# Second half of a feed-forward: weight pairs that move on one by one, stored sums added by accumulating transfers, epilogues in the following visit

## The chip, the cores and the metric

The kernel runs on one core of a Trainium2 chip. The core has a matrix engine (TensorE, PE in the profile, with its weight loads as PEld), VectorE (DVE), ScalarE (ACT), GpSimd (POOL) and SyncE (SP), which here issues nearly all transfers. The metric is the device time of one execution in microseconds; lower is better. The time before is the median of three runs.

## The reference

One layer of a hybrid encoder block: 16 learned tokens are put ahead of 2048 tokens of width 1024; three mixers (a gated linear recurrence, a forgetting attention and an RWKV-7 group) read one input projection and end in one output projection; then comes the feed-forward, which the change is about:

```python
f = causal_dwconv(rms_norm(h, norm_ffn_pre[l]) @ ffn_up[l], ffn_conv[l])
gate, val = jnp.split(f, 2, axis=-1)
f = (jax.nn.gelu(gate, approximate=True) * val) @ ffn_down[l]
h = h + rms_norm(f, norm_ffn_post[l])
```

`ffn_up` is 1024 x 5632, `ffn_down` 2816 x 1024, all in float32; the first 16 rows are dropped at the end.

## The kernel before

The stages follow one another: input projection with the recurrences beside it, attention, output projection (`w_out_tile`), the up half of the feed-forward (`ffn_up`, three passes over 684 tokens each, 22 units a pass), and the down half (class `Down`). Every matrix product is made from a high and a low part of its operands in fp32r: `mm3` (L170) issues three matmuls, high x high, high x low, low x high, on lines 172 to 174. `split` (L1601) makes the parts: ACT copies the high one, DVE or POOL subtracts to get the low one.

**Up.** A unit of `ffn_up` makes 128 gate and 128 value columns with seven products of a Winograd-like scheme. They share three banks of PSUM; `conv` (L1733) reads a finished sum three times, in the bank itself for three of the four outputs, once on ACT (L1736) and twice on DVE (L1738), and `ending` (L1743) multiplies on POOL and stores to the scratch `ff`. `between` (L2137) runs beside each unit: at unit 14 of the last pass (`DOWN_FROM`) it prepares the down weights of the first pair.

**Down.** `ffn_down` has 22 blocks of 128 rows. Twenty of them make ten pairs, k = 0 to 9 (`DOWN_PAIRS`), each worked as 2 x 2 blocks with seven products; the last two blocks (the remaining pair) are multiplied plainly. For a pair, `down_operands` (L1820) loads seven 128 x 512 weight operands, four of them sums kept in the scratch `ds`, and splits each into a slot of 4 KB a partition. Here a set means the seven operands of one pair. Slots: nine in `qp` (the tile `qd` in the profile, kept from the space of the up half's inputs) and 26 in a ring of three pools (tile `dw`, `DOWN_SLOTS`, `DOWN_TURNS`): 35 slots, five sets.

The 2048 tokens make eight blocks of 256. The first half visits every block with pairs 0 to 4, the second half visits every block again with pairs 5 to 9 and the remaining pair. So there are sixteen visits (`Down.pair`, L1867). In each, for each pair, `side` (L1844) loads a 256 x 256 piece of `ff` (tile `u`), POOL makes four sums of 128 x 128 (L1856 to L1859), ACT and DVE split the seven pieces (tile `fo`), and TensorE issues 21 matmuls into seven banks (tile `psd`). Tiles `u` and `fo` have two buffers. At the end of a visit ACT copies three banks (`la`, `rb`, `lb`), DVE makes the sums (L1891 to L1895) and adds the other banks (L1904). `la`, `ra`, `lb`, `rb` and `u2` have one buffer each.

`first` (L1907) stores the four 128 x 512 results to the scratch `part`. `second` (L1914) loads them back (tile `pt`), POOL adds them (L1901), and then `add_normed` (L1510) makes the norm: two squares with row sums on ACT (L1516), the root, then on DVE y x rstd x gain (L1525) and the add to h (L1526); the result goes to `out`. All of this stands at the end of the visit to which it belongs.

The framework orders each engine's instructions with a planner that works from the order of the text and modelled times; `issue_after(ins)` puts instructions behind `ins` in the queue of the same engine. Each engine works its queue in order, and SP's waits hold up the transfers queued behind them.

## Time and profile before

| | us |
|---|---|
| median of three runs | 3062.89 (3059.62 to 3063.98) |
| the profiled execution | 3063.42 |
| its span, first to last instruction | 3061.7 |
| last matmul of the up half starts (in the span) | 2592.2 |
| first matmul of the down half | 2592.3 |
| last matmul of the down half ends | 3050.6 |

The page gives the busy time of each engine over the whole span, and then what each engine did in 40 slices. This line of it shows the load of the transfer engines, in GB/s for each slice; the last six slices are the down half:

```profile
GB/s 216 244 234 207 163 240 292 154 199 205 211 156 92 88 105 211 109 100 122 75 94 206 171 181 180 172 202 213 209 215 212 220 192 165 171 102 175 148 162 145
```

In the views that follow, L172 is line 172 of the kernel, `psd<-dw,fo` is output from inputs, `x416` a count, and a bracket such as `[3.57 <-DVE uy L1738]` is idle time of the engine before the instruction and what ended it. Timelines give start and duration in us from the start of the span.

### The profile page before, as it was taken

What the parts mean: (1) busy time and instruction counts of PE and PEld (TensorE: products, weight loads), DVE (VectorE), ACT (ScalarE), POOL (GpSimd) and SP (SyncE); (2) the same over time, 40 slices, a digit from 0 to 9 for tenths busy, and PEclk for the clock granted to TensorE, in tenths of its full rate; (3) what the DMA queues carried; (4) which work ended last, traced back from release to release, by engine and by line L of the source; (5) the groups of instructions that cost most, each with busy time, mean ns of one, the idle gap of its engine ahead of it and who ended that gap; (6) DMA issues with size and microseconds to landing.
All of it is one profiled execution on the core that took longest, in us unless ns stands there. A gap on an engine that the chain in (4) does not pass through costs nothing.

```text
span 3061.7 us, 52809 instructions
## 1 busy us (share of the span) xinstructions
PE 2910.2 (95%) x18694; PEld 2487.6 (81%) x18694; DVE 2057.7 (67%) x3934; ACT 1479.1 (48%) x2853; POOL 1365.7 (45%) x1599
## 2 busy tenths in 40 slices
PE   6998999999989999999999899999999999999998
PEld 6997898888876654566568899999999999787786
DVE  5268645656677785555636888888778777547766
ACT  4245332434346554454534656666566665324333
POOL 1001121122214556566843457445645544556765
PEclk8999999999989898999999999999999999999999
DMA  6776478466654347434336555566677765535454
GB/s 216 244 234 207 163 240 292 154 199 205 211 156 92 88 105 211 109 100 122 75 94 206 171 181 180 172 202 213 209 215 212 220 192 165 171 102 175 148 162 145
DMA packets 467750, 532.58 MB, mean 174 GB/s; under 512 B 85550, under 2 KB 355576, under 8 KB 465932
## 3 DMA queue, kind: packets, MB, share of 16 engines
q1 hardware_dynamic: 466716, 528.27, 56.5%
q8 instruction: 147, 2.41, 0.3%
q14 instruction: 119, 0.97, 0.1%
q0 software_dynamic: 768, 0.93, 0.1%
HBM read 369.11 MB, written 159.95 MB: 173 GB/s over the span
## 4 chain that ended last, share of the span: by engine, by line
PE 34%; DVE 5%; DMA 5%; POOL 3%; issue 3%; ACT 1%; SPq 0%; POOLq 0%; DVEq 0%; ACTq 0%
PE psu L172 8%; PE psu L173 8%; PE psu L174 8%; PE psd L172 2%; PE psd L173 2%; PE psd L174 2%; DMA u<-scr_ff 2%; DMA xt<-scr_h 1%; DVE uw L1603 1%; PE pswo L172 1%; PE pswo L174 1%; PE pswo L173 1%; DVE fo L1603 1%; DVE uy L1738 1%; POOL u L1858 1%
## 5 line engine op out<-in xcount | busy, mean ns | idle before, releaser
L172 PE MATMUL psu<-xo,uw 128*128 128x344 f32 x1848 | 590.8, 323 | 14.7 <-DVE vb L1787 6.9
L173 PE MATMUL psu<-xo,uw 128*128 128x344 f32 x1848 | 593.1, 321 | 0.0
L174 PE MATMUL psu<-xo,uw 128*128 128x344 f32 x1848 | 584.3, 320 | 1.5 <-DVE uw L1603 1.5
L172 PE MATMUL psp<-xh,wh 128*128 128x384 f32 (+2 forms) x1152 | 383.5, 333 | 4.5 <-ACT wh L166 3.0
L174 PE MATMUL psp<-xh,wl 128*128 128x384 f32 (+2 forms) x1152 | 379.5, 330 | 2.6 <-DMA wl<-scr_wk 2.5
L173 PE MATMUL psp<-xl,wh 128*128 128x384 f32 (+2 forms) x1152 | 379.3, 329 | 0.0
L1603 DVE TENSOR_TENSOR uw<-uq,uw 128x512 fp32r<-128x512 f32 x341 | 321.0, 947 | 65.1 <-ACT uw L1602 62.8
L172 PEld LDWEIGHTS psu<-xo,uw 128*128 128x128 f32 x1848 | 347.4, 189 | 19.2 <-DVE vb L1787 9.4
L174 PEld LDWEIGHTS psu<-xo,uw 128*128 128x128 f32 x1848 | 347.2, 189 | 2.4 <-DVE uw L1603 2.3
L173 PEld LDWEIGHTS psu<-xo,uw 128*128 128x128 f32 x1848 | 348.5, 189 | 0.1
L1602 ACT ACTIVATE uw<-uq 128x512 fp32r<-128x512 f32 x462 | 287.5, 627 | 107.5 <-PE psu L174 46.6
L686 ACT ACTIVATE p<-sc,bias 128x512 f32<-128x512 f32 (+4 forms) x352 | 197.0, 589 | 194.9 <-PE sc L682 162.1
L559 DVE TENSOR_REDUCE mc<-mx 128x1 f32<-128x512 f32 (+6 forms) x352 | 190.2, 564 | 114.1 <-PE mx L554 87.2
L1738 DVE SCALAR_TENSOR_TENSOR uy<-psu,ffn_cols,uy 128x342 f32<-128x342 f32 (+1 forms) x396 | 223.7, 567 | 62.3 <-ACT uy L1736 60.9
L1744 POOL TENSOR_TENSOR uy<-uy,uy 128x342 f32<-128x342 f32 (+1 forms) x132 | 140.0, 1061 | 252.7 <-DVE uy L1738 70.1
L725 POOL TENSOR_TENSOR acc<-acc,p 128x512 f32<-128x512 f32 (+3 forms) x208 | 221.7, 1068 | 53.1 <-DVE acc L725 23.9
L1603 POOL TENSOR_TENSOR uw<-uq,uw 128x512 fp32r<-128x512 f32 x121 | 177.6, 1468 | 148.0 <-ACT uw L1602 129.5
L172 PEld LDWEIGHTS psp<-xh,wh 128*128 128x128 f32 x1152 | 221.7, 192 | 11.6 <-issue 4.2
L174 PEld LDWEIGHTS psp<-xh,wl 128*128 128x128 f32 x1152 | 220.8, 192 | 12.0 <-issue 5.7
L173 PEld LDWEIGHTS psp<-xl,wh 128*128 128x128 f32 x1152 | 221.3, 192 | 7.5 <-issue 5.4
L1603 DVE TENSOR_TENSOR fo<-u,fo 128x896 fp32r<-128x896 f32 x88 | 109.0, 1240 | 118.8 <-ACT fo L1602 118.8
L1602 ACT ACTIVATE fo<-u 128x896 fp32r<-128x896 f32 x88 | 81.1, 922 | 200.9 <-POOL u L1859 103.8
(470 smaller groups left out, 6470.3 us busy)
## 6 DMA issues: line engine op xcount, KB each, us to landing
uq<-scr_us SPq DMA_DIRECT2D x220, 256.0 KB
uq<-in_ffn_up_dram SPq DMA_DIRECT2D x209, 256.0 KB
wl<-scr_wk SPq DMA_DIRECT2D x48, 512.0 KB
wh<-scr_wk SPq DMA_DIRECT2D x48, 512.0 KB
u<-scr_ff SPq DMA_DIRECT2D x88, 256.0 KB
scr_ff<-uy SPq DMA_DIRECT2D x110, 171.0 KB
raw<-in_w_in_dram SPq DMA_DIRECT2D x24, 512.0 KB
scr_wk<-wh SPq DMA_DIRECT2D x24, 512.0 KB
```

What stands on the lines that cost most here:

```text
L172: nc.tensor.matmul(out, ah, bh, start=first, stop=False, skip_group_check=more)
L173: nc.tensor.matmul(out, ah, bl, start=False, stop=False, skip_group_check=more)
L174: nc.tensor.matmul(out, al, bh, start=False, stop=last, skip_group_check=more)
L559: self.reduced = nc.vector.tensor_reduce(mc[:rows, i, ci : ci + 1], ps[:rows, : e - a], axis=AX.X, op=ALU.max)
L686: last = nc.scalar.activation(p[:rows, :w], ps[:rows, :w], AF.Exp, bias=bias[:rows, j : j + 1])
L725: eng.tensor_tensor(a, ps_[0][0][:rows, c0:n] if start and i == 1 else a, p[:rows, : n - c0], op=ALU.add)
L1602: core.nc.scalar.activation(hi, src, AF.Copy)
L1603: (eng or core.nc.vector).tensor_tensor(lo, src, hi, op=ALU.subtract)
L1738: stt(y[:, :n], src[:, i : n + i], cw[:, 44 * i + cc : 44 * i + cc + 1], y[:, :n], op0=ALU.mult, op1=ALU.add)
L1744: core.pooled = nc.gpsimd.tensor_tensor(v[:, :n], g[:, :n], v[:, :n], op=ALU.mult)
L1858: tt(s3, a0, b0, op=ALU.subtract)
```

## The change

Six things change, all at or after the end of the up half.

1. `down_visits`: visit `pair` of the first half works on the five pairs from 5 x pair // 8 on, the second half on the other five, modulo ten. The sets that a visit needs therefore move on by one pair at most from a visit to the next. Fourteen sets are prepared in all (ten before). The following visit's new set is prepared by `ahead`, which is called behind the third side of a visit.
2. 35 slots as before, but ten of them are filled before the down half (three operands of the second pair too, at units 13 and 17 of the last pass): the tenth is the space of `g_fpre`, whose pool `gf` is now opened earlier. The other 25 lie in five pools in another order. The splits of sets 2 and 3 are put behind the last ACT and DVE work of `conv` (`DOWN_HELD`).
3. In the last up unit the sums of two products are written to SBUF tiles instead of to their banks, and the last product is copied to SBUF before `conv`.
4. First half: the stores to `part` are queued behind the load of the fifth following side.
5. Second half: no load of `part`, no adds on POOL. Four transfers issued by POOL add the stored sums onto `la`, `ra`, `lb` and `rb` behind the third following side; norms follow behind the fourth, stores to `out` behind the sixth. The last visit adds the stored sums within its own epilogue. `add_scaled` multiplies by the gain before the root is known, then does (y x rstd) + h in one pass.
6. The remaining pair's weights are loaded in visit 7 (`DOWN_REST`).

```diff
+def add_scaled(core, pool, halves, gain, x, junk):
+
+    nc = core.nc
+    v = pool.tile([P, 8], F32, tag="rs2", name=core.n("rs2"))
+    sums = v[:, 4:5], v[:, 5:6]
+    for y, acc in zip(halves, sums):
+        nc.scalar.activation(junk, y, AF.Square, accum_out=acc)
+    for c, y in enumerate(halves):
+        nc.vector.tensor_tensor(y, y, gain[:, 512 * c : 512 * c + 512], op=ALU.mult)
+    r1 = rstd_root(core, v, sums, D)
+    for c, y in enumerate(halves):
+        xc = x[:, 512 * c : 512 * c + 512]
+        nc.vector.scalar_tensor_tensor(xc, y, r1, xc, op0=ALU.mult, op1=ALU.add)
...
-DOWN_SLOTS = 5, 13, 8
-DOWN_TURNS = (2, 3), (0, 5), (1, 13), (2, 5)
-DOWN_FROM = 14
+DOWN_SLOTS = 5, 7, 1, 2, 10
+DOWN_TURNS = (3, 2), (4, 5), (0, 5), (4, 5), (1, 7), (2, 1)
+DOWN_FROM = 13, 17
+DOWN_HELD = 2, 4
+DOWN_REST = 6
+DOWN_AHEAD = 2
+DOWN_STORED = 5
+DOWN_PARTS, DOWN_NORMS, DOWN_OUT = 3, 4, 6
...
             elif name == "p3":
-                tt(ps, ps, u2, op=ALU.add)
-                gb = conv(ps, 0, j, n[1])
+                sum_ = ps if more else u2
+                tt(sum_, ps, u2, op=ALU.add)
+                gb = conv(sum_, 0, j, n[1])
...
             elif name == "p2":
-                tt(ps, ps, ga, op=ALU.add)
-                ga = conv(ps, 0, j, n[0])
+                sum_ = ps if more else ga
+                tt(sum_, ps, ga, op=ALU.add)
+                ga = conv(sum_, 0, j, n[0])
...
             else:
-                va = conv(ps, 1, j, n[0])
+                src = ps
+                if not more:
+                    src = s("ga")
+                    nc.scalar.activation(src, ps, AF.Copy)
+                va = conv(src, 1, j, n[0])
...
+def down_visits(pairs):
+
+    for half in range(2):
+        for pair in range(pairs):
+            first = DOWN_CUT * pair // pairs + DOWN_CUT * half
+            yield half, pair, range(first, first + DOWN_CUT)
...
+        self.sides += 1
+        while self.due and self.due[0][0] <= self.sides:
+            with core.tc.issue_after(load.ins):
+                self.due.pop(0)[1]()
+        return side
...
-        for k in ks:
-            side, w = self.side(k, pair), weights(k)
+        for i, k in enumerate(ks):
+            if i == DOWN_AHEAD:
+                self.due.insert(0, (self.sides + 1, ahead))
+            side, w = self.side(k % DOWN_PAIRS, pair), weights(k)
...
-        for i, row in enumerate(((lb, rb), (la, ra)) if rest else ()):
-            t0 = P * (2 * pair + i)
-            pt = self.spool.tile([P, D], F32, tag="hx", name=core.n("pt"))
-            nc.sync.dma_start(pt[:], self.scr["part"][t0 : t0 + P, :])
-            for c, y in enumerate(row):
-                nc.gpsimd.tensor_tensor(y, y, pt[:, 512 * c : 512 * c + 512], op=ALU.add)
+        out = (la, ra), (lb, rb)
+        if between:
+            between(*out)
...
+        self.after(DOWN_STORED, lambda: store(1, a))
+        self.after(DOWN_STORED, lambda: store(0, b))
...
+        def parts(*ab):
+            for i, halves in zip((1, 0), ab):
+                t0 = P * (2 * pair + i)
+                for c, y in enumerate(halves):
+                    part = self.scr["part"][t0 : t0 + P, 512 * c : 512 * c + 512]
+                    nc.gpsimd.dma_start(y, part, accum_op=ALU.add)
+
+        a, b, junk = self.pair(pair, ks, weights, ahead, rest, parts if ends else None)
...
+        def norms():
+            for t0, halves in rows:
+                hx = self.spool.tile([P, D], F32, tag="hx", name=core.n("hx"))
+                nc.sync.dma_start(hx[:], self.scr["h"][META + t0 : META + t0 + P, :])
+                add_scaled(core, self.spool, halves, self.gain, hx, junk)
+                sums[t0] = hx
...
+        if not ends:
+            self.after(DOWN_PARTS, lambda: parts(a, b))
+        self.after(DOWN_NORMS, norms)
+        self.after(DOWN_OUT, stores)
...
+            def ahead(pair=pair, half=half, ks=ks, last=following[2][-1]):
+                if last not in ks:
+                    weights(last)
+                if half == 0 and pair == DOWN_REST:
+                    for i in range(2):
+                        rest.append(dwn.tile([P, 2, D], F32R, tag=f"r{i}", name=core.n("dwn")))
+                        at = P * (2 * DOWN_PAIRS + i)
+                        load_parts(core, (dpo, "hx", None), a["ffn_down"][at : at + P, :], rest[i][:, 0], rest[i][:, 1])
```

More of the change, by code (lines that the diff above doesn't have):

```diff
@@ L2193, in hybrid_block_kernel @@
+        down[:0] = [dws[i] for i, n in DOWN_TURNS for _ in range(n)]
         steps = Down(core, dpo, dpf, dpe, ps_d, scr, g_fpost, out)
         pairs = SEQ // (2 * P)
[L2195 to L2203 removed]
@@ L2215, in hybrid_block_kernel, with weights @@
-        rest = []
-        for pair in range(pairs):
-            steps.second(pair, ks[1], weights, last)
+        ended = core.taken.ins, core.conved.ins
+        def weights(c):
+            have = ws.setdefault(c, [])
+            if len(have) < len(DOWN_PRODUCTS):
+                raw = lambda: dwr.tile([P, 512], F32, tag="dq", name=core.n("raw"))[:]
+                with ExitStack() as behind:
+                    for ins in ended if c in range(*DOWN_HELD) else ():
+                        behind.enter_context(tc.issue_after(ins))
+                    some = range(len(have), len(DOWN_PRODUCTS))
+                    have += down_operands(core, raw, slot, a["ffn_down"], scr, c % DOWN_PAIRS, some)
+            return have
@@ new lines, in hybrid_block_kernel @@
+        rest = []
+        def last():
+            return rest
+        visits = list(down_visits(pairs))
+        for (half, pair, ks), following in zip(visits, visits[1:] + visits[-1:]):
+            def ahead(pair=pair, half=half, ks=ks, last=following[2][-1]):
[6 more added lines that the diff above has]
+                        load_parts(core, (dpo, "hx", None), a["ffn_down"][at : at + P, :], rest[i][:, 0], rest[i][:, 1])
+            if half == 0:
+                steps.first(pair, ks, weights, ahead)
+                if pair == 1:
+                    gain = a["norm_ffn_post"].rearrange("(o n) -> o n", o=1).broadcast_to([P, D])
+                    nc.sync.dma_start(g_fpost[:], gain)
+            else:
+                steps.second(pair, ks, weights, ahead, last, (half, pair, ks) == visits[-1])
@@ L2220 @@
+        steps.finish()
 def kernel(**inputs):
```

122 lines of the change are left out of this document (58 added, 64 removed).

## The prediction

> **What bounds the kernel now.** I read the totals first, then the second half of the feed-forward cut into its visits. A visit is one of the 16 passes of the down projection over 256 tokens; the first eight take 105 matmuls each (5 weight pairs, 7 products, 3 matmuls), the last eight 129 (24 more for the remaining pair of row blocks). The view of windows below is cut at visit 1, visits 2 to 7, visit 8, visit 9, visits 10 to 16, and the tail after the last matmul. Its columns are window, length, then busy time of each engine with its count, granted clock, DMA share and rate.
>
> ```profile
> PE 2910.2 (95%) x18694; PEld 2487.6 (81%) x18694; DVE 2057.7 (67%) x3934; ACT 1479.1 (48%) x2853; POOL 1365.7 (45%) x1599
> 2592.00:2628.20 36.20, 29.78 (x109) 21.81 (x107) 25.45 (x28) 20.22 (x33) 22.19 (x25) 0.86 0.75 250
> 2628.20:2774.30 146.10, 145.43 (x631) 118.66 (x632) 70.56 (x82) 39.47 (x51) 76.96 (x122) 1.00 0.32 107
> 2774.30:2799.50 25.20, 24.68 (x106) 19.31 (x104) 21.84 (x22) 14.27 (x24) 20.10 (x20) 1.00 0.62 206
> 2799.50:2837.60 38.10, 32.78 (x129) 25.93 (x130) 32.31 (x34) 18.27 (x29) 27.94 (x31) 0.91 0.55 179
> 2837.60:3050.60 213.00, 210.23 (x904) 168.66 (x903) 147.63 (x192) 72.28 (x136) 143.87 (x165) 1.00 0.47 155
> 3050.60:3061.70 11.10, 0.00 (x0) 0.00 (x0) 6.59 (x14) 2.40 (x8) 0.76 (x1) 0.59 0.38 142
> ```
>
> TensorE bounds the kernel, here as elsewhere. Visits 2 to 7 are six times 105 matmuls in 146.1 us, 0.2319 us each, with PE busy throughout: that is the pace at which nothing is missing. At it a visit of the first half takes 24.35 us, one of the second half 29.9. So the losses are: visit 1, 36.2 - 24.35 = 11.85; visit 8, 0.85; visit 9, 38.1 - 29.9 = 8.2; visits 10 to 16, 213.0 - 7 x 29.9 = 3.6. Together 24.5 us, which is all that a rearrangement of these visits can win, plus something of the 11.1 us tail. The number of matmuls does not change.
>
> Visit 1, in the timeline of PE:
>
> ```profile
> 2592.79 0.40 PE L174 MATMUL psd<-qd,fo 128*128 128x512 f32 x1
> 2596.76 0.77 PE L172 MATMUL psd<-qd,fo 128*128 128x512 f32 x1 [3.57 <-DVE uy L1738]
> ...
> 2599.72 0.76 PE L172 MATMUL psd<-qd,fo 128*128 128x512 f32 x1 [1.34 <-DVE uy L1738]
> 2600.29 0.63 PE L173 MATMUL psd<-qd,fo 128*128 128x512 f32 x1
> ...
> 2604.98 0.63 PE L172 MATMUL psd<-qd,fo 128*128 128x512 f32 x1
> 2605.71 0.39 PE L174 MATMUL psd<-qd,fo 128*128 128x512 f32 x1
> ```
>
> Two banks of PSUM are still being read by the convolutions of the last up unit (4.9 us of waiting), and then 11 matmuls from 2600.29 to 2604.98 start 0.426 us apart: half clock. Seventeen such matmuls, at 0.194 above the pace, cost 3.3 us. The remaining 3.65 us are weights and sides that come late.
>
> **The change, part by part.** *Start-up.* In the last up unit the two sums now go to SBUF tiles and the last product is copied there, so a bank is held for one add or one copy, not for a scaling and two more passes. Rows of the tile psu in the stretch from 2570 to 2600:
>
> ```profile
> L1738 DVE SCALAR_TENSOR_TENSOR uy<-psu,ffn_cols,uy x14: 558/566/574, 2569.8 to 2599.0; 128x342 f32<-128x342 f32 x10, 128x338 f32<-128x338 f32 x4
> L1736 ACT ACTIVATE uy<-psu,ffn_cols x6: 522/530/545, 2573.6 to 2593.2; 128x342 f32<-128x342 f32 x4, 128x338 f32<-128x338 f32 x2
> L1768 ACT ACTIVATE u<-psu x2: 458/458/458, 2571.2 to 2584.2; 128x344 f32<-128x344 f32 x2
> L1790 DVE TENSOR_TENSOR psu<-psu,ga x2: 515/520/524, 2574.7 to 2590.2; 128x344 f32<-128x344 f32 x2
> ```
>
> Each of three banks comes free 0.53 + 2 x 0.57 = 1.67 us of work earlier, against one more copy of 0.46, which lies under the matmuls; with ACT and DVE queues in between I take both waits as gone, and with them the slow stretch. Then weights become the limit. Ten of the 35 operands of visit 1 are now ready before it (seven before), and the remaining pair's load (two transfers of 512 KB) leaves the rush:
>
> ```profile
> 2596.00:2608.00 12.00, 9.89 (x27) 7.43 (x28) 8.34 (x11) 7.22 (x11) 5.74 (x5) 0.60 0.92 314
> L1602 ACT ACTIVATE dw<-raw x26: 612/629/637, 2589.7 to 2618.3; 128x512 fp32r<-128x512 f32 x26
> L1603 DVE TENSOR_TENSOR dw<-raw,dw x18: 678/692/1781, 2590.9 to 2619.1; 128x512 fp32r<-128x512 f32 x18
> L1603 POOL TENSOR_TENSOR dw<-raw,dw x8: 1259/1294/1721, 2594.0 to 2620.3; 128x512 fp32r<-128x512 f32 x8
> L166 ACT ACTIVATE dwn<-raw x2: 1056/1056/1057, 2601.6 to 2603.6; 128x1024 fp32r<-128x1024 f32 x2
> L167 DVE TENSOR_TENSOR dwn<-raw,dwn x2: 1226/1226/1226, 2602.7 to 2604.7; 128x1024 fp32r<-128x1024 f32 x2
> ```
>
> In that window the transfers run at a 0.92 share and 314 GB/s: they are the limit. Three operands of 256 KB and two of 512 KB are 1.84 MB, 5.8 us at that rate; 2.1 us of ACT and 2.5 of DVE go with them, in the same queues. So the weights come 5.8 us earlier, and a little more where the ACT or DVE queue was the holder: I take 6.5 of the 11.85. Ends: 0 (the weights were late anyhow) and 11.85.
>
> The Trainium skill (TensorE: Matmul & The Clock Gate, "Part 1: The HAM clock gate") has the clock fall after an idle window of about 3.4 us. By that rule any remaining wait shorter than that is free of the slow stretch, and visit 1 could win 3.3 us more. Visit 9 disagrees: there waits of 2.81 and 1.31 us, the first for ACT, bring the granted clock to 0.72 in the 12 us from 2800. So I do not count on it.
>
> ```profile
> 2800.00:2812.00 12.00, 8.42 (x24) 6.36 (x25) 12.00 (x13) 8.28 (x15) 10.97 (x12) 0.72 0.86 281
> 2802.27 0.50 PE L172 MATMUL psd<-qd,fo 128*128 128x512 f32 x1 [2.81 <-ACT fo L1602]
> 2804.79 1.22 PE L174 MATMUL psd<-qd,fo 128*128 128x512 f32 x2 [1.31 <-DVE fo L1603]
> ```
>
> *The seam.* Before, all five sets of weights are exchanged while visits 8 and 9 run: DVE is busy 12.00 of 12 us in the window above, and the sides (fo) queue behind 25 splits. Now each visit replaces at most one set: prepared in visits 2, 4, 5, 7, 8, 10, 12, 13 and 15, nine sets, four more than before (28 operands, 7 MB). Such a set takes seven ACT splits, 7 x 0.629 = 4.4 us, five on DVE, 3.5 to 8.9, and two on POOL, 2.6. Its slots come free after the first pair of the visit and it is wanted at the last pair of the next one, some 40 us later, so arrival is not the question; delay of the sides in the queues is. In the first half DVE has 70.56 / 6 = 11.8 us of 24.35: room. Bounds for one set: 0, and the 0.85 of visit 8, in which a first part of the sets was prepared. I take 0.3, nearer to visits 2 to 7, whose DVE has twice the room that visit 8 had: 5 x 0.3 = 1.5 us in the first half.
>
> *The second half.* Visits 10 to 16 lose 0.5 each, through this chain (tables of waits of PE's loads and of DVE from 2838 to 3051):
>
> ```profile
> PEld psd L172 <- ACT fo L1602: 6.7, 11, 1.0
> DVE ra L1904 <- POOL ra L1901: 8.8, 7, 1.4
> L1901 POOL TENSOR_TENSOR la<-la,pt x8: 1293/1738/1747, 2836.1 to 3043.9; 128x512 f32<-128x512 f32 x8
> L2041 POOL DMA_DIRECT2D scr_p<-zeros x12: 537/537/720, 1.3 to 10.4; - x12
> DMA to landing us min/median/max: 2.9/5.7/6.7
> ```
>
> The stored sums are added by POOL, about 1.74 + 3 x 1.27 = 5.6 us a visit (the smaller value is a row of the tail, below), between the adds that make the sides; DVE waits for them, and ACT's split waits for both. The change takes these adds off POOL and puts four accumulating transfers in their place. No such transfer is in the trace. The nearest are POOL's twelve small stores at the start: 0.54 us to issue, 2.9 to 6.7 to land. So POOL gives 2.2 us in place of 5.6. The norms move into the next visit, behind its fourth side. Same operations in number, but there DVE has to fit a weight set too: 147.63 / 7 = 21.1 us a visit, plus 3.5 to 8.9, of 29.9. That eats what the shorter chain gives, so I leave 0.5 us of loss in each of the eight visits, visit 9 now included: 4.0 in place of 11.8, -7.8 us. Ends: 0 lost (-11.8), and nothing won beyond the seam's own 8.2 given back by crowded visits (0).
>
> *The tail.* The last visit cannot spread its epilogue. Rows of POOL, DVE and SP:
>
> ```profile
> 3050.09 1.27 POOL L1901 TENSOR_TENSOR rb<-rb,pt 128x512 f32<-128x512 f32 x1
> 3051.40 0.69 DVE L1904 TENSOR_TENSOR rb<-rb,psd 128x512 f32<-128x512 f32 x1
> 3056.97 0.69 DVE L1526 TENSOR_TENSOR hx<-hx,rb 128x512 f32<-128x512 f32 x1
> ```
>
> Before, rb is complete at 3052.1. Now its transfer is issued about 3049.5 and lands 2.9 to 6.7 later, 3052.4 to 3056.2, and DVE's add follows: 1 to 4.8 us late. In return the gain is multiplied in while ACT squares, and the other row is finished by then; from 3052.1 to 3057.7 the old chain interleaves both rows in 5.6 us, the new one needs about 3 after rb. Between -1.6 and +2.2: I take 0.
>
> *Sum.* -6.5 (visit 1) - 0.85 (visit 8) - 7.8 (second half) + 1.5 (sets) + 0 (tail) = -13.65 us. The profiled execution took 3063.42 us (its span 3061.7 and 1.7 around it): 3049.8. The median of the runs is 0.53 lower, so 3049.2.
>
> **Rivals.** *Sets that crowd every visit.* Each of nine sets costs visit 8's 0.85, 7.65, and visit 1 wins only the bank waits, 4.9: -4.9 - 0.85 - 7.8 + 7.65 = -5.9, 3057. For it: DVE at up to 30.0 of 29.9 us in visits 10, 12, 13 and 15. Against: 40 us of lead.
>
> *Late accumulations; slower.* la, ra, lb and rb have one buffer each, and ACT's four squares of 0.63 us must wait for the transfers, with the split of the fifth side behind them. From the start of a visit: sums complete at about 2 (three adds of 0.69), issues to 4.2, and the fifth side is needed at 4 x 4.87 = 19.5. Less 2.5 of squares, 0.95 of ACT and 1.3 of DVE for the side, landing is free until 14.7, that is 10.5 us after issue: beyond the 6.7 seen. But if each issue is held by a DVE instruction of 1.32 (a side's split), issues end at 9.4 (2 + 4 x 1.86), and landing after 5.3 us costs. At 6.7 it is 1.4 us in seven visits, 10 us: 3059; at 9, 3.7 each, 26 us: 3075. Slower than before it is from 7.3 us on, where seven times 2.0 undo the sum. I price it at 9. For it: POOL's adds of a side take 0.45 at least and up to 1.3, and the transfers are eight times the twelve stores' size (256 KB). Against: those stores landed after 6.7 at worst. Rows of the squares, the sides and POOL's adds in the second half:
>
> ```profile
> L1516 ACT ACTIVATE u<-la x8: 631/632/637, 2839.0 to 3049.6; 128x512 f32<-128x512 f32 x8
> L1602 ACT ACTIVATE fo<-u x41: 632/952/955, 2841.4 to 3040.3; 128x896 fp32r<-128x896 f32 x34, 128x512 fp32r<-128x512 f32 x7
> L1603 DVE TENSOR_TENSOR fo<-u,fo x41: 692/1322/2183, 2843.1 to 3041.0; 128x896 fp32r<-128x896 f32 x34, 128x512 fp32r<-128x512 f32 x7
> L1858 POOL TENSOR_TENSOR u<-u x33: 452/1307/1315, 2842.8 to 3036.3; 128x128 f32<-128x128 f32 x33
> ```
>
> The Trainium skill (SBUF — State Buffer, the warning on "DVE blocks DMA") says that descriptors of POOL's transfers wait while DVE holds the shared port pair in a two-port operation; no run here shows it yet for a transfer.
>
> *It does not do what it says.* The instruction order is made by a planner: the remaining pair's splits stand at 2601.6, though the text puts them in visit 9. If sets are placed late, each costs a fifth of the seam, 9.05 / 5 = 1.8, and nine cost 16.3: -6.5 - 0.85 - 7.8 + 16.3 = +1.1, 3064.
>
> **How the numbers follow.** My forecast 0.60 (own range 3041 to 3056), crowding 0.17, late accumulations 0.13, misplaced sets 0.10. About 0.2%, 6.1 us, is what can be told from no change. Faster: 0.60 and a little over half of crowding, 0.70. Same: the rest of crowding and most of the misplaced sets, 0.16. Slower 0.14. The low end is all 24.5 us won, 3038; the high end takes in most of the late accumulations, 3067.
>
> **What would show it.** The same cut into visits: visit 1 near 30 us with no wait for uy and fewer slow matmuls; visits 8 and 9 near 25 and 30.4; visits 10 to 16 near 213; tail near 11. Wrong would be: visits 10 to 16 above 220 with ACT's squares waiting for a transfer (late accumulations), or visits 2 to 7 above 150 (crowding).

## The result, and the profile after

The change makes the kernel slower: 3076.8 us in the median (3066.49 to 3077.64, six runs) against 3060.01 (3059.04 to 3063.98, six runs) on the same chip; the ratio estimated from these runs is 1.0046, with a 95% interval of 1.0033 to 1.0058. The forecast of 3049.2 had the sign wrong, and the time lies above the range's end of 3067. The profiled execution took 3071.23 us, its span is 3069.5. The page's totals and its line for the software queue, in which the accumulating transfers go (before, that queue moved 0.93 MB in 0.1% of the time):

```profile
PE 2913.2 (95%) x18694; PEld 2484.8 (81%) x18694; DVE 2055.7 (67%) x3954; ACT 1495.5 (49%) x2882; POOL 1347.8 (44%) x1607
q0 software_dynamic: 5376, 9.32, 1.7%
```

The totals hardly differ, so the answer has to come from the stage. The same view of windows as before the change, cut at the first matmul of visits 1, 2, 3, 8, 9, 10 and at the last matmul:

```profile
2588.40:2618.80 30.40, 27.12 (x106) 18.76 (x105) 22.89 (x25) 20.59 (x35) 21.70 (x20) 1.00 0.81 271
2618.80:2647.60 28.80, 26.55 (x107) 20.80 (x106) 18.60 (x22) 10.49 (x16) 16.18 (x24) 0.94 0.45 146
2647.60:2769.50 121.90, 121.28 (x527) 98.51 (x526) 73.47 (x82) 46.35 (x63) 72.50 (x105) 1.00 0.44 149
2769.50:2794.00 24.50, 24.45 (x107) 19.56 (x106) 17.11 (x19) 10.43 (x15) 16.16 (x22) 1.00 0.51 172
2794.00:2823.60 29.60, 29.60 (x130) 24.22 (x129) 16.47 (x21) 6.98 (x9) 16.36 (x24) 1.00 0.30 97
2823.60:3056.90 233.30, 215.64 (x904) 172.03 (x902) 148.45 (x206) 85.86 (x162) 128.52 (x171) 0.98 0.62 178
3056.90:3069.50 12.60, 0.38 (x2) 0.00 (x0) 7.58 (x15) 3.21 (x10) 0.00 (x0) 0.72 0.39 115
```

Visit 1 is short, visits 8 and 9 run at the pace, visits 3 to 7 as before. Visits 10 to 16 take 233.3 us instead of 213.0. Set against 0.2319 us a matmul, from the starts of the matmuls in the trace (so that a single visit can be told; the cuts differ by some tenths from those of the windows in the prediction), the losses in us are:

| | visit 1 | 2 to 7 | 8 and 9 | 10, 12, 13, 15 (a set is prepared) | 11, 14, 16 (none) | after the last matmul |
|---|---|---|---|---|---|---|
| before | 11.5 | -0.1 | 9.2 | 1.8 | 1.5 | 11.3 |
| after | 6.1 | 4.5 | -0.1 | 19.8 | 4.3 | 12.4 |

The sixteen visits thus lose 10.7 us more than before, and 1.1 come with the tail. Visit 1 begins 3.9 us earlier (2588.4 instead of 2592.3): in this execution the up half's first matmul came 6.3 us earlier (1675.7 instead of 1682.0), and the up half took 2.4 us longer. Together that is 7.9, the difference of the spans within rounding. The 6.3 lie in stages that the change does not touch. Over all profiled executions of this study that start moves between 1675.7 and 1692.9, so kernels are compared below by ratios of many runs and by their visits, not by one execution's span. Without the 6.3 us the two profiles differ by 14.1, which is what the ratio makes of 3060 us.

In the changed kernel a new set's weights are loaded on L1870 (tile `raw`, a weight as it was loaded) and split on L1619 (high part, ACT) and L1620 (low part); a side is loaded on L1891, summed on L1901 to L1904 and split on L1619 too; L1537 is the norm's square, L1980 the accumulating transfer.

What the engines wait for in visits 10 to 16 (engine and line, what ended the wait, us in total, times, longest): PE before the change, then ACT and PE after it, and the rows of the new transfers with the time they took to land:

```profile
PE psd L172 <- ACT fo L1602: 2.7, 6, 0.5
```

```profile
ACT fo L1619 <- POOL u L1904: 41.3, 14, 4.1
ACT u L1537 <- DMA la<-scr_part: 31.5, 7, 6.5
PE psd L172 <- ACT fo L1619: 17.6, 10, 3.6
```

```profile
L1980 POOL DMA_DIRECT2D la<-scr_part x8: 884/884/931, 2822.5 to 3050.9; - x8
L1980 POOL DMA_DIRECT2D ra<-scr_part x8: 971/1180/1219, 2823.1 to 3051.7; - x8
L1980 POOL DMA_DIRECT2D lb<-scr_part x8: 861/1144/1548, 2826.2 to 3053.3; - x8
L1980 POOL DMA_DIRECT2D rb<-scr_part x8: 1139/1204/1294, 2827.3 to 3053.9; - x8
DMA to landing us min/median/max: 3.7/8.0/10.0
```

Before, PE waited 2.7 us in these visits. Now it waits 17.6 us for the splits of sides (fo). ACT, which makes them, stands idle for 31.5 us because the square of la is at the head of its queue and la's accumulation has not landed. This is what the prediction named as the sign of late accumulations. Visit 12, which lasts from 2888.7 to 2924.4, shows how; ACT first, then SP:

```profile
2888.92 0.96 ACT L1619 ACTIVATE fo<-u 128x896 fp32r<-128x896 f32 x1 [2.15 <-PE psd L174]
2896.36 0.63 ACT L1537 ACTIVATE u<-la 128x512 f32<-128x512 f32 x1 [6.49 <-DMA la<-scr_part]
...
2900.54 0.63 ACT L1619 ACTIVATE dw<-raw 128x512 fp32r<-128x512 f32 x1 [0.71 <-DMA raw<-in_ffn_down_dram]
2901.07 0.93 ACT L1619 ACTIVATE fo<-u 128x896 fp32r<-128x896 f32 x1
...
2908.08 0.95 ACT L1619 ACTIVATE fo<-u 128x896 fp32r<-128x896 f32 x1 [3.56 <-POOL u L1904]
```

```profile
2888.43 0.46 SPq L1870 DMA_DIRECT2D raw<-in_ffn_down_dram  x1
...
2893.22 0.90 SPq L1891 DMA_DIRECT2D u<-scr_ff  x1
2894.16 1.11 SPq L1989 DMA_DIRECT2D hx<-scr_h  x2
2903.16 7.49 SPq L1891 DMA_DIRECT2D u<-scr_ff  x2
```

ACT splits the second side at 2888.92. Next in its queue are la's square, five of the new set's seven splits and ra's square, and only then, at 2901.07, the third side's split. That side has been ready since 2894.8, when POOL ended its last sum; PE gets it at 2902.06, after 3.56 us of waiting. The fourth side's load is issued at 2893.22, behind the seven raw weights. By its 256 packets of 1 KB in the trace it lands at 2903.3, 10.1 us later; its split follows at 2908.08. Between the two, the transfer engines are full:

```profile
2889.00:2893.00 4.00, 4.00 (x19) 3.26 (x18) 2.38 (x4) 0.87 (x1) 3.77 (x6) 1.00 0.74 215
2893.00:2897.00 4.00, 4.00 (x20) 3.26 (x19) 0.00 (x0) 0.64 (x3) 1.77 (x3) 1.00 1.01 241
2897.00:2901.00 4.00, 1.50 (x7) 0.90 (x5) 3.65 (x5) 3.29 (x8) 1.41 (x1) 1.00 1.10 261
2901.00:2906.00 5.00, 3.94 (x10) 3.16 (x11) 4.29 (x8) 2.96 (x7) 2.71 (x3) 0.66 0.99 366
```

The last two columns are the busy share of the 16 engines and GB/s. The queues between 2893 and 2901 (packets, MB, share of the 16 engines in these 8 us):

```profile
q0 software_dynamic: 502, 0.93, 63.3%
q1 hardware_dynamic: 587, 1.08, 42.1%
```

0.93 MB of accumulation take 0.633 x 8 = 5.1 us of all engines, 184 KB/us; SP's 1.08 MB take 3.4 us, 320 KB/us. An accumulated byte here costs 1.7 times a loaded one, and the two classes share the engines. (The shares add up to 105%, since packets overlap.) Four transfers, seven raws, three side loads and two rows of h make up the 4.7 MB that move from 2889 to 2906.

The prediction left open whether DVE's work holds up POOL's transfers. It does not explain the lateness here. By the packets in the trace, data of la's transfer begin to move 1.58 to 1.62 us after its issue in visits 11, 14 and 16, and 2.94 to 3.31 us after it in visits 10, 12, 13 and 15. DVE does the same adds of banks on L1957 beside the issue in all seven; what differs is that SP has just issued the new set's raws. Once under way, the transfers moved 0.41 MB from 2893 to 2897 with DVE at 0.00 of 4 us and 0.52 MB in the next 4 us with DVE at 3.65. So the rule of the Trainium skill (SBUF — State Buffer, the warning on "DVE blocks DMA") is not what makes these visits late; whether DVE's operations here were of the two-port kind that it speaks of, no view tells.

### The profile page after: what moved, and what is told of

The parts are those of the page before. It is cut to its first block, busy times and chain, and to the rows that moved or that the text cites. A ratio compares the mean times of both kernels' runs of the same rounds, so it can differ in the third digit from the quotient of the medians.

```text
span 3069.5 us, 52923 instructions
## 1 busy us (share of the span) xinstructions
PE 2913.2 (95%) x18694; PEld 2484.8 (81%) x18694; DVE 2055.7 (67%) x3954; ACT 1495.5 (49%) x2882; POOL 1347.8 (44%) x1607
## 4 chain that ended last, share of the span: by engine, by line
PE 34%; DMA 6%; DVE 4%; POOL 2%; issue 2%; ACT 1%; SPq 1%; DVEq 0%; POOLq 0%; ACTq 0%
PE psu L172 8%; PE psu L173 8%; PE psu L174 8%; PE psd L172 2%; PE psd L173 2%; PE psd L174 2%; DMA xt<-scr_h 1%; PE pswo L172 1%; PE pswo L174 1%; PE pswo L173 1%; DMA u<-scr_ff 1%; DMA raw<-in_ffn_down_dram 1%; DVE uw L1620 1%; DMA raw<-scr_ds 1%; DVE fo L1620 1%
## 5 line engine op out<-in xcount | busy, mean ns | idle before, releaser
L1620 DVE TENSOR_TENSOR uw<-uq,uw 128x512 fp32r<-128x512 f32 x341 | 321.1, 948 | 67.0 <-ACT uw L1619 64.7
L1619 ACT ACTIVATE uw<-uq 128x512 fp32r<-128x512 f32 x462 | 287.0, 627 | 106.1 <-PE psu L174 46.3
L1620 POOL TENSOR_TENSOR uw<-uq,uw 128x512 fp32r<-128x512 f32 x121 | 178.5, 1475 | 150.3 <-ACT uw L1619 122.6
L172 PEld LDWEIGHTS psp<-xh,wh 128*128 128x128 f32 x1152 | 218.2, 189 | 11.6 <-issue 4.0
L1619 ACT ACTIVATE fo<-u 128x896 fp32r<-128x896 f32 x88 | 81.0, 921 | 184.5 <-POOL u L1904 98.6
L1620 DVE TENSOR_TENSOR fo<-u,fo 128x896 fp32r<-128x896 f32 x88 | 100.9, 1146 | 101.4 <-ACT fo L1619 100.9
```

Source lines behind the costliest of these rows:

```text
L172: nc.tensor.matmul(out, ah, bh, start=first, stop=False, skip_group_check=more)
L1619: core.nc.scalar.activation(hi, src, AF.Copy)
L1620: (eng or core.nc.vector).tensor_tensor(lo, src, hi, op=ALU.subtract)
```

## The experiments

Two theories stood at the start. T: ACT's squares wait for transfers that land late, with the sides' splits behind. S: the moved sets crowd the visits. Twelve kernels ran; ratios are to the kernel before on the same chip, with 95% intervals. The losses and landings are those of one profiled execution of each. The losses per visit are worked out as above; landing is the longest time from issue to the last packet of a side's load in that set's visit, for visits 10, 12, 13, 15.

| kernel | ratio | 1 | 2 to 7 | 8, 9 | 10, 12, 13, 15 | 11, 14, 16 | tail | landing |
|---|---|---|---|---|---|---|---|---|
| before | | 11.5 | -0.1 | 9.2 | 1.8 | 1.5 | 11.3 | 3.1, 3.6, 3.7, 3.6 |
| after | 1.0046 | 6.1 | 4.5 | -0.1 | 19.8 | 4.3 | 12.4 | 10.4, 10.1, 9.6, 10.1 |
| e1_loads | 1.0106 [1.0071, 1.0140] | 5.7 | 4.0 | -0.4 | 43.9 | 2.6 | 11.6 | 7.1, 6.2, 7.0, 6.8 |
| e2_no_parts | 0.9926 [0.9905, 0.9947] | 6.7 | 4.4 | -0.4 | 1.0 | -0.8 | 9.6 | 4.5, 4.2, 4.4, 4.6 |
| e3_hold | 1.0040 [1.0019, 1.0060] | 5.7 | 6.0 | -0.4 | 18.1 | 5.0 | 14.2 | 9.8, 9.8, 9.3, 9.8 |
| e4_fixed | 1.0079 [1.0052, 1.0106] | 6.3 | -0.2 | 10.9 | 17.0 | 13.2 | 13.5 | 3.5, 6.3, 4.6, 6.0 |
| e5_old_end | 1.0035 [1.0017, 1.0052] | 7.1 | 2.6 | 1.6 | 21.4 | -0.1 | 12.0 | 5.4, 5.2, 5.9, 6.3 |
| e6_aside | 1.0109 [1.0076, 1.0142] | 5.8 | 40.3 | 10.3 | 3.6 | -0.8 | 9.7 | 4.5, 3.6, 4.1, 5.0 |
| e7_early_late | 0.9988 [0.9970, 1.0005] | 6.0 | 4.1 | -0.4 | 12.4 | -0.7 | 17.0 | 10.0, 8.8, 9.8, 9.1 |
| e8_ahead4 | 1.0110 [1.0080, 1.0140] | 5.7 | 12.3 | 2.7 | 19.1 | 18.2 | 12.5 | 6.4, 6.1, 6.5, 6.8 |
| e9_three_u | 0.9949 [0.9928, 0.9970] | 6.0 | 6.0 | -0.4 | 1.0 | -0.5 | 12.7 | 7.1, 7.5, 7.1, 7.4 |
| e10_three_u_held | 0.9942 [0.9925, 0.9959] | 6.0 | 3.8 | -0.4 | -1.1 | -0.5 | 15.6 | 4.6, 7.9, 7.5, 7.4 |
| e11_aside_plain | 0.9983 [0.9966, 1.0000] | 6.1 | 16.7 | 4.7 | 1.6 | -0.8 | 9.7 | 4.0, 4.4, 4.9, 3.7 |
| e12_spread | 1.0027 [1.0012, 1.0041] | 6.1 | 8.3 | 0.9 | 15.7 | 0.3 | 17.2 | 6.6, 6.2, 8.1, 6.4 |

(e4_fixed has no set in visits 10 to 16; the planner places every instruction anew in each kernel, so neighbouring things shift a little too.)

**The accumulating transfers replaced, e1_loads.** SP loads the sums and POOL adds them, at the same place:

```diff
-                for c, y in enumerate(halves):
-                    part = self.scr["part"][t0 : t0 + P, 512 * c : 512 * c + 512]
-                    nc.gpsimd.dma_start(y, part, accum_op=ALU.add)
+                pt = self.spool.tile([P, D], F32, tag="hx", name=core.n("pt"))
+                nc.sync.dma_start(pt[:], self.scr["part"][t0 : t0 + P, :])
+                for c, y in enumerate(halves):
+                    nc.gpsimd.tensor_tensor(y, y, pt[:, 512 * c : 512 * c + 512], op=ALU.add)
```

> The changed kernel with the stored sums brought in as before: two plain loads issued by SP and four adds on POOL, at the same place in the text (behind the third following side). Everything else stays, the moving weight sets too. Theory T (transfers): ACT's queue holds the squares of the norm ahead of the splits of two sides, and waits there for accumulating transfers that take 8 us; this costs about 20 of the 24.1 us that visits 10 to 16 lose. Then this kernel loses at most 6 us in them and takes about 3077 - 20 = 3057 us. Rival S (sets): the four visits in which a weight set is prepared (10, 12, 13, 15 carry 19.8 of the 24.1 us) are crowded on ACT and DVE whatever brings the sums. Then the visits still lose 15 us or more: above 3068 us.

It is slower than the change, and by the expectation's count that speaks for S: 46.5 us are lost in visits 10 to 16, 43.9 of them in the four with a set. But the trace shows another road than S or T had in mind. In visit 12 POOL's four adds stand in its queue behind the new set's two splits and ahead of the fourth side's sums; POOL, then ACT and PE:

```profile
2918.25 2.14 POOL L1981 TENSOR_TENSOR la<-la,pt 128x512 f32<-128x512 f32 x1
...
2923.73 1.70 POOL L1981 TENSOR_TENSOR rb<-rb,pt 128x512 f32<-128x512 f32 x1
2925.40 0.90 POOL L1901 TENSOR_TENSOR u<-u 128x128 f32<-128x128 f32 x1
...
2931.15 1.79 ACT L1619 ACTIVATE fo<-u 128x896 fp32r<-128x896 f32 x2 [2.19 <-POOL u L1904]
2932.15 0.80 PE L172 MATMUL psd<-dw,fo 128*128 128x512 f32 x1 [9.57 <-ACT fo L1619]
```

The adds take 7.2 us, and PE waits 9.57 us. ACT's squares wait for the adds as well (23.3 us for la in the seven visits), but the split that PE misses waits for POOL's sums. So late sums cost time without any accumulating transfer too, here in POOL's queue and not in ACT's, and this run does not decide between the theories.

**The sums left out, e2_no_parts.** The call in `parts` becomes `pass`, so the stored sums of the first half are not added; sets and norms stay.

> The changed kernel without the adding of the stored sums: the four transfers of each visit of the second half are left out, so the result lacks the first half's sums. Theory T: visits 10 to 16 lose at most 4 us and the tail is about 3 us shorter: about 3053 us. Rival S: they still lose 15 us or more: above 3066 us.

```profile
2835.30:3044.70 209.40, 208.21 (x904) 169.24 (x902) 154.02 (x211) 86.94 (x164) 109.58 (x140) 1.00 0.47 160
```

Visits 10 to 16 run at the pace, 209.4 us. Moving sets and late norms cost nothing there by themselves; S, the prediction's crowding, falls for these visits. The loss goes with the sums, as T had it.

**The squares held, e3_hold.** They are queued behind the fourth side's split, where the prediction had put them:

```diff
 def split(core, hi, lo, src, eng=None):
-    core.nc.scalar.activation(hi, src, AF.Copy)
+    core.hi = core.nc.scalar.activation(hi, src, AF.Copy)
...
-                add_scaled(core, self.spool, halves, self.gain, hx, junk)
+                with core.tc.issue_after(core.hi.ins):
+                    add_scaled(core, self.spool, halves, self.gain, hx, junk)
```

> The changed kernel with one edge more: the norm's instructions on ACT are queued behind the split of the side at which the text puts them (the fourth), where the planner had moved the first squares ahead of the third and fourth sides and of a set's splits. Transfers and sets stay. Theory T: the wait for the transfers then stands where the sides are already split; visits 10 to 16 lose 5 to 10 us in place of 24.1, about 3077 - 16 = 3061 us. Rival S: no change, 3074 us or more. If instead the norms now come too late for the next visit's first copies (one buffer each), the loss moves to the start of the visits, with PE waiting behind ACT la, and the time stays above 3070 us.

A miss for T as stated: nothing is won. The squares no longer wait, but the new set's splits now do, for their raw weights, and they stand ahead of the third side's split as the squares did. Visit 12 of this kernel, ACT:

```profile
2902.95 0.63 ACT L1619 ACTIVATE qd<-raw 128x512 fp32r<-128x512 f32 x1 [2.24 <-DMA raw<-in_ffn_down_dram]
2904.05 0.63 ACT L1619 ACTIVATE qd<-raw 128x512 fp32r<-128x512 f32 x1 [0.47 <-DMA raw<-scr_ds]
2906.96 0.63 ACT L1619 ACTIVATE kd<-raw 128x512 fp32r<-128x512 f32 x1 [2.28 <-DMA raw<-scr_ds]
...
2912.63 0.63 ACT L1619 ACTIVATE dw<-raw 128x512 fp32r<-128x512 f32 x1 [1.33 <-DMA raw<-in_ffn_down_dram]
2913.17 0.93 ACT L1619 ACTIVATE fo<-u 128x896 fp32r<-128x896 f32 x1
```

That side was ready at 2909.4, and PE waits 4.82 us for it. The lateness is thus not one of the squares alone: while the transfer engines are full, raws and sums both land late, and in both kernels one of them stands in ACT's queue ahead of a side.

**Halves that do not move, e4_fixed.** The first half keeps pairs 0 to 4, the sets are exchanged at the seam:

```diff
-            first = DOWN_CUT * pair // pairs + DOWN_CUT * half
+            first = DOWN_CUT * half
...
-                if last not in ks:
-                    weights(last)
+                for c in range(last + 1 - DOWN_CUT, last + 1):
+                    if c not in ks:
+                        weights(c)
```

> The changed kernel with fixed halves as before: pairs 0 to 4, then 5 to 9, all five sets exchanged between visits 8 and 9, none in visits 10 to 16. Transfers and late norms stay. Theory T: visits 10 to 16 still lose 1 to 2.8 us each, about 10 us together (the visits without a set, 11, 14 and 16, lost 2.4, 1.0 and 0.9), and the seam returns with about 9 us; about 3077 - 14 + 9 - 4 (visits 1 to 7 without sets) = 3068 us. Rival S: visits 10 to 16 lose 3 to 4 us as before the change, 3061 us.

Slower again: the seam's loss is back (10.9). Both expectations were too low for visits 10 to 16: T had reckoned with about 10 us, S with 3 to 4, and they lose 30.2, 4.3 each, without any set. The sets are thus not necessary for a loss. ACT and PE from visit 11 on:

```profile
ACT u L1537 <- DMA lb<-scr_part: 23.4, 6, 4.2
PE psd L172 <- ACT fo L1619: 15.9, 6, 3.1
```

Here the square of lb stands ahead of the third side's split and starts 10.2 to 11.4 us after a visit's first matmul, while PE wants that side after 9.7 us. In the changed kernel's visits without a set, 11, 14 and 16, the order is the same; there lb's square starts after 10.4, 7.0 and 9.0 us, and they lose 2.4, 1.0 and 0.9. The sets cost something in the first half: visits 2 to 7 lose 4.7 us less here.

**The old end of a visit, e5_old_end.** Loads by SP, adds by POOL, norms and stores at the end of the same visit; start-up, slots and moving pairs as changed:

```diff
-        a, b, junk = self.pair(pair, ks, weights, ahead, rest, parts if ends else None)
+        a, b, junk = self.pair(pair, ks, weights, ahead, rest, parts)
...
-        if not ends:
-            self.after(DOWN_PARTS, lambda: parts(a, b))
-        self.after(DOWN_NORMS, norms)
-        self.after(DOWN_OUT, stores)
+        norms()
+        stores()
```

(`parts` is that of e1_loads.)

> The changed kernel with the old end of a visit in its second half: SyncE loads the stored sums, GpSimd adds them at the visit's end, squares, norm and store follow at once; start-up, kept banks and the moving pairs stay as changed. Theory W (the loss lies in the late sums, with squares ahead of the sides' splits): visits 10 to 16 lose as before, 0.3 to 0.7 us each, seam and visit 1 keep their gains of 9.3 and 5.4 us, visits 2 and 7 their losses of 3.6 and 1.1: 9 to 11 us below before, some 3050 on a chip where before takes 3060. Theory B (the transfers' traffic beside the sets' loads): the same, since the same bytes come over SyncE's queue at another moment; if the sets themselves cost, about before's time.

A miss: 21.4 us are lost in the four visits with a set, none in the others. The old chain of adds and squares, which cost 0.3 to 0.7 us a visit before, costs 5.3 us as soon as a set is prepared in the same visit; and sets without sums cost nothing in e2_no_parts.

**The transfers where nobody waits, e6_aside, and as copies, e11_aside_plain.** Both leave the sums of the first half out of the result.

```diff
-                    nc.gpsimd.dma_start(y, part, accum_op=ALU.add)
+                    aside = self.scr["aside"][t0 : t0 + P, 512 * c : 512 * c + 512]
+                    nc.gpsimd.dma_start(aside, part, accum_op=ALU.add)
```

This is e6_aside; e11_aside_plain is the same without `accum_op=ALU.add`.

> Each of the four accumulating transfers of a visit reads the same stored rows at the same place, but adds them to rows in memory that nobody reads, so that nothing waits for them; the sums of the first half are left out of the result. Traffic and GpSimd's issues stay, the wait is gone. Theory W (wait for late sums): visits 10 to 16 lose under 1 us each, time as without the sums, about 3047 where before takes 3063. Theory B (the transfers fill the DMA engines and hold up raw weights and sides): visits 10 to 16 still lose over 12 us in all, mostly those with a set (10, 12, 13, 15), time over 3060.

> As the run that sent the transfers to rows nobody reads, but copying in place of accumulating; the sums of the first half are left out of the result. D: a copied row takes the DMA engines a third to a half of what an accumulated one takes (some 390 KB/us as SyncE's loads of 2 to 4 KB pieces move, instead of 100 to 170), the side's loads land in 5 us instead of 7 to 9, and the 48 us that visits 2 to 9 lost fall under 20. If it is the issue on GpSimd (1.2 us each ahead of the sides' sums) or the way over the software queue, the loss stays above 35.

Without a dependence on la the planner issued all 32 transfers in visits 2 to 9, so visits 10 to 16, of which e6_aside's expectation speaks, are no test of it, and the places compared are these: with accumulation they lose 50.6 us, with copies 21.4 (theory D, that the transfers fill the engines and so make the sides' loads late, had said under 20, its rivals over 35), in the changed kernel 4.4. No one waits for these transfers, and still they cost about 46 us, more than 5 us for four, while visits 10 to 16, now without them, are nearly free. In visits 3 to 6 of e6_aside the last side's load takes 7.0 to 8.1 us to land, in e11_aside_plain 3.4 to 4.1. That it is the load and not the issuing on POOL that holds the side shows in visit 4 of e6_aside: POOL has issued all four and then stands idle until the load has landed:

```profile
2723.79 0.45 POOL L1902 TENSOR_TENSOR u<-u 128x128 f32<-128x128 f32 x1 [6.03 <-DMA u<-scr_ff]
```

So traffic alone, with nobody waiting for it, can delay a side. The software queue in the stretch of the transfers, first with accumulation (225 us), then with copies (210 us):

```profile
q0 software_dynamic: 4488, 8.19, 25.5%
```

```profile
q0 software_dynamic: 2560, 8.39, 13.0%
```

57.4 us of all engines for 8.19 MB, and 27.3 us for 8.39 MB: 143 against 307 KB/us. The copies also go in larger pieces (3.3 KB against 1.8) and are issued in 0.52 us instead of 1.16, so the share of adding alone in the factor of two is not told apart.

**Other places, e7_early_late, e8_ahead4 and e12_spread.**

The first edit is e8_ahead4's. The second, with the squares held as in e3_hold, is e7_early_late's; e12_spread adds `DOWN_AHEAD = 3` to it.

```diff
-DOWN_AHEAD = 2
+DOWN_AHEAD = 4
```

```diff
-DOWN_PARTS, DOWN_NORMS, DOWN_OUT = 3, 4, 6
+DOWN_PARTS, DOWN_NORMS, DOWN_OUT = 2, 5, 6
```

> Transfers one side earlier (second side instead of third, where the set's loads are), norms one side later (fifth) with their squares queued behind that side's split. If W and B together make the loss, visits 10 to 16 lose under 1.5 us each (8 us in all instead of 24): 3052 to 3056 where before takes 3063. W alone gives 3050. If the transfers cost their 3 to 4 us a visit wherever they stand (as with fixed halves), 3068.

> The set of the next visit is loaded and split two sides later (fifth instead of third), the transfers and norms stay. B: the raws no longer meet the transfers, the 24 us of visits 10 to 16 fall to 10 or less, about 3060 where before takes 3063. W: the squares still stand ahead of the fourth side's split at a place the planner picks, so 15 us or more stay, 3068 or more.

> Transfers at the second side, the set at the fourth, norms at the fifth with the squares behind its split; two side buffers. D: the transfers have landed before the seven raws start, so no side's load lands later than 6 us; visits 10 to 16 lose under 5 us in all instead of 24 (12 with the set at the third side). If a late set costs by itself, as with the set at the fifth side, 15 or more.

Transfers one side earlier and norms one later win half of the loss, less than expected (11.7 us stay, not 8): visits 12 and 15 lose 0.9 each, 10 and 13 still 3.5 and 7.2, and the tail grows by 4.6 us. Taking the set away from the transfers is a miss both times. With the set two sides later (e8_ahead4) visits 10 to 16 lose 37.3, with and without a set alike, and visits 2 to 7 lose more too (12.3 in place of 4.5). One side later (e12_spread, to be compared with e7_early_late) 16.0 us stay in visits 10 to 16, and ACT again waits for raw weights, 7 us at once:

```profile
ACT qd L1619 <- DMA raw<-in_ffn_down_dram: 9.7, 2, 6.7
ACT dw L1619 <- DMA raw<-in_ffn_down_dram: 8.1, 3, 7.0
```

In these kernels spreading the traffic is not enough; the set's splits have to stand somewhere in ACT's queue, and a side stands behind them.

**One more side in stock, e9_three_u and e10_three_u_held.** By now the theory, D, was: the transfers fill the transfer engines and so make the loads late, and two buffers for `u` leave only one side of 4.87 us in stock against it.

```diff
-DOWN_RAWS = 8
+DOWN_RAWS = 7
...
-        u = self.fpool.tile([P, 8, P], F32, tag="u", name=core.n("u"))
+        u = self.fpool.tile([P, 8, P], F32, tag="u", name=core.n("u"), bufs=3)
```

(The third buffer, 4 KB a partition, needs the room of one raw. e10_three_u_held adds e7's places and the held squares.)

> The changed kernel with three buffers for a side's load instead of two (and seven raw buffers instead of eight), so that a load can stand a side further ahead; transfers, norms and sets as changed. Theory D (the transfers fill the 16 DMA engines, a side's load behind the seven raws lands after 10 us instead of 3, and the matmuls wait for that side): a side more of lead, 4.9 us, covers most of it, visits 10, 12, 13, 15 lose 1 to 2 us instead of 5 to 6, visits 10 to 16 under 9 in all instead of 24. Theory W (the squares wait for the sums in ScalarE's queue, with the third side's split behind): the lead is of no use, the split still stands behind the squares, 18 us or more stay.

> Three side buffers, transfers at the second side, norms at the fifth with the squares behind its split. D and W together: neither the late load nor the squares reach the matmuls; visits 10 to 16 lose under 3 us in all (21.5 less 12 in the whole stretch), 0.996 of before or less. If the transfers cost PE time by another road (GpSimd's queue, where each is issued), the seven visits keep 8 us or more and the ratio stays near the 0.999 of the run with two buffers.

Visits 10 to 16 lose 0.5 and -1.5 us in all instead of 24.1. Of e9_three_u, the stretch of these visits and the waits in it:

```profile
2839.80:3049.50 209.70, 208.22 (x904) 169.28 (x902) 150.39 (x206) 86.50 (x163) 130.80 (x167) 1.00 0.69 188
```

```profile
ACT u L1537 <- DMA la<-scr_part: 26.2, 7, 5.3
PE psd L172 <- ACT fo L1619: 1.5, 2, 1.3
```

ACT still stands 26.2 us before la's square, a side's load still takes over 7 us, and the transfer engines are busier than in the changed kernel (0.69 against 0.62). PE waits 1.5 us. So here neither the late sum nor the late load costs by itself; what decides is whether the matmuls have a side left when it comes. The buffer does more than hold one side longer, though. SP waits less before it issues a side's load (112.8 us in these visits for the splits that free a buffer, instead of 141.7), and what is queued behind it goes earlier too: in visit 12 the set's first raw is issued 8.2 us before the visit's first matmul instead of 0.3, four of the seven splits now stand ahead of la's square, and the third side's split starts 10.1 us after the visit's start instead of 12.4. How much is the stock and how much this order, and what the one raw less does, no run tells apart. Both kernels are faster than the kernel before: e10_three_u_held takes 3053.24 us where before takes 3073.28, a gain of 0.58% (0.41 to 0.75), e9_three_u 3056.17. What a third buffer would do to the kernel before was not tried; its visits 10 to 16 have 3.3 us to give.

## Why the prediction was wrong, step by step

For the profiled execution the forecast was 3049.8 us; it took 3071.23, 21.4 more. The terms below, measured less forecast, make 25.3 of it: visit 1 1.1, seam -0.7, sets 3.2, second half 20.6, tail 1.1. The up half, for which the sum had no term, adds 2.4, and 6.3 go off for the earlier stages. (In the twelve other kernels the up half takes 910.6 to 915.1 us against 910.3 before, so that part of the 2.4 may be chance.)

- *Visit 1: right.* -6.5 forecast, -5.4 measured, both waits for `uy` gone, the granted clock 1.00 instead of 0.86; late weights remain, as said.
- *Seam: right.* Visits 8 and 9 were to win 8.55 (0.85 + 8.2 less the 0.5 left to visit 9) and won 9.3. They now run at the pace.
- *Sets in the first half, +1.5: too small.* Visits 2 to 7 lose 4.7 more, 3.6 of it in visit 2. They take 150.7 us, just above the 150 that the prediction had named as the sign of crowding; but that rival priced every set at 0.85, and of the four visits in which sets are prepared there, only 2 and 7 lose (3.6 and 1.1; 7 also loads the remaining pair's weights), 4 and 5 nothing. The rows of visit 2 have the same pattern as the second half (ACT, PE, and a window of 5 us):

```profile
2621.35 0.63 ACT L1619 ACTIVATE qd<-raw 128x512 fp32r<-128x512 f32 x1 [2.38 <-DMA raw<-in_ffn_down_dram]
2624.73 0.93 ACT L1619 ACTIVATE fo<-u 128x896 fp32r<-128x896 f32 x1
```

```profile
2623.44 0.50 PE L172 MATMUL psd<-qd,fo 128*128 128x512 f32 x1 [0.94 <-DVE la L1957]
2625.71 0.80 PE L172 MATMUL psd<-qd,fo 128*128 128x512 f32 x1 [1.32 <-ACT fo L1619]
2624.00:2629.00 5.00, 3.68 (x10) 2.62 (x9) 5.00 (x6) 2.65 (x5) 3.54 (x2) 0.66 0.21 73
```

  A split of the set waits for its raw, the second side's split stands behind, PE waits for it and then works at a mean granted clock of 0.66. No run was aimed at this visit. The error was "so arrival is not the question": early arrival for PE says nothing about splits that wait in ACT's queue ahead of something more urgent.
- *Tail: 0 forecast, +1.1 measured*, inside its bounds of -1.6 and +2.2.
- *Second half: the step that failed.* "I leave 0.5 us of loss in each of the eight visits" stood for visits 10 to 16 at 3.5 us; they lost 24.1. Three things in it were off. First, the sizes: the landing was taken from small stores, at most 6.7 us, and is 8.0 in the median; the issue was taken as 0.54 and is 0.88 to 1.2 in the medians of the four. Second, the transfers were counted as work taken from POOL and never as load on the 16 transfer engines, where 1.05 MB a visit hold all engines some 5.7 us (at the 184 KB/us above) just when raws and sides are wanted. Third, the 0.5 was argued from DVE's busy time, while the trace shows the sides held in ACT's queue, behind a square or a split that waits for a transfer, with one side in stock.
- *The rival that came true, late accumulations*, had a chance of 0.13, and its own price of 3075 us lay above the end of the stated range. Its place was half right. It put the squares behind the fourth side's split, with landing free until 14.7 us after the start of a visit. In the trace la's square stands behind the second side's split, and the third side is wanted 9.7 us after the start. Holding the squares where the rival had put them (e3_hold) won nothing, so its mechanism as worked out, squares alone, is not the whole: raws and side loads are late by the same traffic. At 8 us its formula gives 2.7 x 7 = 19 us; the 20.8 measured (24.1 less the 3.3 before) agree in size, but by luck, since the formula counts from another place in the queue. "Slower than before it is from 7.3 us on" fits a median of 8.0 in a slower kernel; one kernel does not test the threshold.
- *Crowding and misplaced sets*: sets cost nothing in visits 10 to 16 when no sums are added (e2_no_parts); together with the sums they do, since in the changed kernel visits with a set lose 5.0 each and the others 1.4. Sets alone are thus not the cause; e4_fixed shows that the transfers cost without sets, e5_old_end that sets with the old chain of sums cost without the accumulating transfers.

What stays open: why lb's sum lands later in e4_fixed than in visits 14 and 16 of the changed kernel, and how the loss divides between the waits in the queues and the loads that the traffic delays.

## What to carry to other kernels

Moving a sum from an engine to an accumulating transfer moves its cost to the transfer engines; price it there, per byte, in the few microseconds in which the other loads of the loop are issued, not over the span. When work is spread into the next stage, look at each in-order queue for what late thing will stand at its head, and for how many microseconds of operands are in stock behind it. Where no order helps, one more buffer for the operand that the bound engine eats may be worth more than re-ordering: here 4 KB a partition turned +0.46% into -0.5%, and none of the four re-orderings (e3_hold, e7_early_late, e8_ahead4, e12_spread) came clearly below the kernel before.

## What the runs showed of the hardware

- Accumulating transfers of 256 KB: issue on POOL 0.88 to 1.2 us each in the medians, landing after 3.7, 8.0 and 10.0 us (least, median, most), 184 KB/us of all 16 engines against 320 for SP's loads beside them. From memory to memory 143 against 307 KB/us for copies.
- Waits of PE of 2.85, 3.47 and 3.56 us (visits 13, 15 and 12) were followed by a mean granted clock of 0.66 over 5 us, waits of 1.88 and 2.33 us (visits 10 and 11) by 1.00; 0.94 and 1.32 us in visit 2, 2.3 us apart, were followed by 0.66 again. The loss of visits 10 to 16 is larger than PE's waits in them: 24.1 against 17.6 us.
